# A chain of layers on one core: norms between layers on VectorE alone, their root read from PSUM, and table set-up in smaller steps

## The chip, the core and the metric

The kernel runs on one core of a Trainium2 chip. A core has five engines with instruction queues of their own: PE (TensorE, matrix products), DVE (VectorE) and ACT (ScalarE) for elementwise work, POOL (GpSimd), and SP, which issues DMA transfers. They meet through semaphores. PE writes to PSUM, which DVE and ACT can read and POOL cannot; everything else lies in SBUF. The metric is the time of one execution in microseconds, the median of three runs. PE's clock has two levels, 1.2 and 2.4 GHz; the profile gives the granted clock as a share of full speed.

## The reference

Two blocks of two layers each run one after the other on a sequence of 512 tokens with 1024 channels in float32: a pooling mixer, a gated feed-forward layer with a short convolution (ffn0), windowed attention, a second such feed-forward layer (ffn1), a state-space layer (s5), an MLP (mlp0), a second kind of state-space layer (ssd), an MLP (mlp1) and a last norm. What matters here is what lies between them:

```python
def rms_norm(x, g):
    y = xf * lax.rsqrt(jnp.mean(xf * xf, axis=-1, keepdims=True) + RMS_EPS)
    return y * g
# first block, twice: a norm before, a norm behind
    h = rms_norm(x, mix_pre_g[layer])
    x = x + rms_norm(m, mix_post_g[layer])
    f = conv_glu_ffn(rms_norm(x, ffn_pre_g[layer]), ...)
    x = x + rms_norm(f, ffn_post_g[layer])
# second block, twice: a norm with scale and shift before
    h = _modulate(_rmsnorm(x, norm_mix_g[i]), sh1, sc1)      # h * (1 + scale) + shift
    x = x + g1 * y
    h = _modulate(_rmsnorm(x, norm_mlp_g[i]), sh2, sc2)
    x = x + g2 * _sq_relu_mlp(h, mlp_w1[i], mlp_w2[i])
```

The s5 layer needs tables that depend only on its parameters (powers of complex numbers, phasors, small matrices), and the second block needs modulation vectors (`mod`), products of a condition vector with large matrices.

## The kernel before, in words

The state `xT` is kept transposed: eight tiles of 128 channels x 512 tokens in SBUF. A product with a weight matrix is made of three matmuls (lines 219 to 221): every float32 operand is split into a rounded high part and a low part (ACT writes the high part, DVE the difference), and high x high, high x low and low x high are added up in PSUM. A weight chunk of 128 x 1024 is loaded by SP and split likewise (lines 204 and 205).

**Passages.** `seam` (line 796) joins two layers. For each half of the tokens it issues the last products of the old layer (`tail`), then, with high priority, the chain between them (`chain`, and `run` of the pre-norm), then the first products of the new layer (`head`). There are seven such passages: pool to ffn0, ffn0 to attention, attention to ffn1, ffn1 to s5, s5 to mlp0, mlp0 to ssd and ssd to mlp1.

**Norms.** `Norm.add` (line 283) squares a tile on ACT and adds it to a sum of squares; there are two sums, one added up by DVE and one by POOL, shared out by `engs(k)` (odd tiles to POOL). `Norm.rs` (line 298) takes the sum over channels with matmuls against ones (line 306, both sums accumulated), makes the root on ACT (309) and the reciprocal on DVE (310), spreads it over diagonal matrices (313) and by matmuls over all partitions (319), and copies the result from PSUM to SBUF on ACT (321). The PSUM pool for this, `psn`, has one buffer. `Norm.rs` is called 22 times: eleven norms, two halves.

`post_add` (line 438) is the norm behind a layer of the first block: product with root and gain (lines 449 and 450), addition to `xT` (453), and, where the next layer is of the kind `PreScale`, the split of the result (427, 428), which needs no root since the root is multiplied in after the product. Tiles 2 and 5 are multiplied on POOL (their gain is multiplied in ahead by ACT, line 442), and odd tiles are added on POOL. `PreNorm.run` (line 26) is the norm before a layer of the second block: product with the root (397, alternately on DVE and POOL), scale and shift on DVE (400), rounding on ACT (401), and low part on DVE (402). `staged` issues such steps in a skewed order that `POST_LAGS` and `PRE_LAGS` set.

**Background.** Tables for s5 (`s5_tables`, `s5_powers`, lines 535 to 662), their last part (`s5_toeplitz`) and the modulation (`vecmat`) are generators. `bg[0](n)` takes n steps of each; a step ends at a `yield`. During pool one step is taken behind the first half (line 932). The layer ffn0 takes four steps as its body begins (`bg[0](rate)`, line 998) and four after each pair of column tiles, one after each evacuation of a down projection, and what is left at its end. The layer ffn1 does the same with a rate of three, for the modulation and the last part of the tables.

**Order.** The instructions are written in program order, but a planner that simulates the program sets the order on each engine: by readiness and by priority, which is the place in the program order unless it is raised. Where an engine would be idle in the simulation, it is given later work that is ready. On the chip each engine then runs its queue strictly in that order.

Of the kernel before, what the change touches and what calls it, by code (L numbers as in the profile page):

```python
# [11 lines left out]
F32 = mybir.dt.float32  # L12
# [9 lines left out]
P = 128  # L22
# [9 lines left out]
POST_LAGS = (0, 2, 3, 4)  # L32
PRE_LAGS = (0, 1, 1, 3)
POOL_K = (2, 5)
# [29 lines left out]
def net_kernel(ctx: ExitStack, tc: tile.TileContext, I: dict, out: bass.AP, parts=ALL):  # L64
# [213 lines left out]
    class Norm:  # L278
        def __init__(self):
            self.acc = {}  # L280
            self.seen = set()

        def add(self, tile_, span, eng):
            a, b = span
            if eng not in self.acc:
                self.acc[eng] = tt("acc")
            dst = self.acc[eng][:, a:b]
            if (eng, a) not in self.seen:
                self.seen.add((eng, a))
                if span == FULL:  # L290
                    self.seen.add((eng, HALVES[1][0]))
# [6 lines left out]
        def rs(self, span, eps, out=None):  # L298
# [3 lines left out]
            accs = list(self.acc.values())  # L302
# [11 lines left out]
            if nb == 2:  # L314
                p2 = ps[:, 256:]
            else:
                p2 = psn.tile([P, 512], F32, tag="n", name=nm("pn"))
# [53 lines left out]
    class PreNorm:  # L371
# [15 lines left out]
        def run(self, span):  # L387
# [25 lines left out]
    class PreScale(PreNorm):  # L413
# [21 lines left out]
    def engs(k):  # L435
        return G if k % 2 else V
# [1616 lines left out]
```

## Time and profile before

| | |
|---|---|
| median of three runs | 2519.96 us (2519.84 to 2521.32) |
| profiled execution: its own time | 2522.2 us |
| its span, first to last instruction | 2520.5 us |
| mean granted clock of PE | 0.968 |
| busy: PE, DVE, ACT, POOL | 94%, 68%, 46%, 18% of the span |
| instructions | 33869 |

The busy shares are means over stages with different limits. PE is busy nearly throughout, so what counts is where it stands still or runs at the lower clock, and who is late there. The granted clock falls below 1 in and behind the passages between layers. A row of a timeline gives the start, the time taken by the row's instructions together, the engine, line and operands, and in brackets the idle time of the engine just before, with what ended it. An instruction's duration includes a tail in which the next one can already run, so the distance between two starts is its price where an engine works without a break.

### The profile page before, as it was taken

What the parts mean: (1) busy time and instruction counts of PE and PEld (TensorE: products, weight loads), DVE (VectorE), ACT (ScalarE), POOL (GpSimd) and SP (SyncE); (2) the same over time, 40 slices, a digit from 0 to 9 for tenths busy, and PEclk for the clock granted to TensorE, in tenths of its full rate; (3) what the DMA queues carried; (4) which work ended last, traced back from release to release, by engine and by line L of the source; (5) the groups of instructions that cost most, each with busy time, mean ns of one, the idle gap of its engine ahead of it and who ended that gap; (6) DMA issues with size and microseconds to landing.
All of it is one profiled execution on the core that took longest, in us unless ns stands there. A gap on an engine that the chain in (4) does not pass through costs nothing.

```text
span 2520.5 us, 33869 instructions
## 1 busy us (share of the span) xinstructions
PE 2358.8 (94%) x12485; PEld 1986.4 (79%) x12485; DVE 1717.7 (68%) x2969; ACT 1151.8 (46%) x2070; POOL 454.9 (18%) x489
## 2 busy tenths in 40 slices
PE   6889999988889999996899999999999999999998
PEld 5767777876677888886878887788877888888888
DVE  6895987677858778777654666666778788633333
ACT  6443534467676444354543432333555554422322
POOL 2202131131321000014111210112133432301110
PEclk9989999989999999997999999999999999999999
DMA  4234443312094555551952356543333332233322
GB/s 123 67 100 131 125 138 112 122 43 67 27 231 136 176 175 167 184 176 56 304 158 76 114 167 195 178 149 97 110 101 97 111 103 82 91 100 97 96 88 72
DMA packets 297782, 311.32 MB, mean 124 GB/s; under 512 B 53569, under 2 KB 251025, under 8 KB 296593
## 3 DMA queue, kind: packets, MB, share of 16 engines
q1 hardware_dynamic: 270033, 278.22, 35.5%
q10 hardware_dynamic: 23680, 17.31, 2.3%
q0 software_dynamic: 3904, 13.63, 1.6%
q8 instruction: 98, 1.61, 0.3%
q14 instruction: 67, 0.55, 0.1%
HBM read 284.92 MB, written 24.18 MB: 123 GB/s over the span
## 4 chain that ended last, share of the span: by engine, by line
PE 70%; DVE 12%; DMA 7%; ACT 5%; issue 4%; POOL 1%; SPq 0%; DVEq 0%; ACTq 0%; POOLq 0%
PE mm L220 20%; PE mm L219 20%; PE mm L221 20%; DMA as<-in_ada_w 4%; DVE wl L205 2%; DVE aa L504 1%; DMA tz<-d_k 1%; ACT wh L204 1%; PE pb L1725 1%; PE mm L1655 1%; DVE u L450 1%; PE mm L1656 1%; PE mm L1657 1%; PE pn L306 1%; PE pb L765 1%
## 5 line engine op out<-in xcount | busy, mean ns | idle before, releaser
L219 PE MATMUL mm<-h,wh 128*128 128x512 f32 (+1 forms) x1792 | 665.0, 374 | 40.5 <-DVE u L952 14.2
L220 PE MATMUL mm<-h,wh 128*128 128x512 f32 (+1 forms) x1792 | 668.3, 374 | 24.8 <-DVE h L428 12.6
L221 PE MATMUL mm<-h,wl 128*128 128x512 f32 (+1 forms) x1792 | 665.7, 372 | 1.9 <-DVE wl L205 1.9
L204 ACT ACTIVATE wh<-ws 128x1024 fp32r<-128x1024 f32 (+1 forms) x367 | 387.6, 1059 | 563.7 <-PE mm L220 490.4
L205 DVE TENSOR_TENSOR wl<-ws,wh 128x1024 fp32r<-128x1024 f32 (+1 forms) x367 | 467.2, 1277 | 256.0 <-ACT wh L204 247.6
L219 PEld LDWEIGHTS mm<-h,wh 128*128 128x128 f32 x1792 | 348.0, 195 | 97.6 <-issue 16.9
L220 PEld LDWEIGHTS mm<-h,wh 128*128 128x128 f32 x1792 | 348.3, 195 | 83.6 <-DVE h L428 15.5
L221 PEld LDWEIGHTS mm<-h,wl 128*128 128x128 f32 x1792 | 348.9, 195 | 57.0 <-DVE wl L205 2.5
L219 PE MATMUL mm<-hi,wh 128*128 128x512 f32 (+1 forms) x1056 | 370.9, 356 | 10.1 <-ACT wh L204 9.6
L220 PE MATMUL mm<-lo,wh 128*128 128x512 f32 (+1 forms) x1056 | 371.9, 354 | 1.6 <-DVE lo L328 1.5
L221 PE MATMUL mm<-hi,wl 128*128 128x512 f32 (+1 forms) x1056 | 371.0, 353 | 0.2 <-DVE wl L205 0.2
L219 PEld LDWEIGHTS mm<-hi,wh 128*128 128x128 f32 x1056 | 201.3, 191 | 37.8 <-ACT wh L204 10.9
L220 PEld LDWEIGHTS mm<-lo,wh 128*128 128x128 f32 x1056 | 202.2, 191 | 28.4 <-DVE lo L328 2.6
L221 PEld LDWEIGHTS mm<-hi,wl 128*128 128x128 f32 x1056 | 201.4, 191 | 26.8 <-DVE wl L205 0.7
L504 DVE SCALAR_TENSOR_TENSOR aa<-as,cond,aa 128x512 f32<-128x512 f32 x168 | 130.5, 777 | 113.3 <-DMA as<-in_ada_w 112.1
L1279 POOL TENSOR_TENSOR r<-r 128x512 f32<-128x512 f32 x64 | 85.7, 1343 | 520.1 <-ACT r L1275 445.3
L771 POOL TENSOR_TENSOR dd<-ident,s5dg 16x64 f32<-16x64 f32 x16 | 56.6, 3539 | 327.5 <-DVE kt L773 320.3
L296 POOL TENSOR_TENSOR acc<-acc,sq 128x256 f32<-128x256 f32 (+1 forms) x64 | 58.5, 916 | 302.8 <-ACT sq L295 292.4
L328 DVE TENSOR_TENSOR lo<-r,hi 128x512 fp32r<-128x512 f32 x64 | 47.2, 743 | 76.9 <-ACT hi L326 76.9
L1300 DVE SCALAR_TENSOR_TENSOR x<-mm,mod,x 128x512 f32<-128x512 f32 (+1 forms) x76 | 48.9, 662 | 62.5 <-PE mm L221 62.4
L512 ACT ACTIVATE ab<-aa 128x512 bf16<-128x512 f32 x72 | 45.0, 625 | 89.5 <-DVE aa L504 49.8
L326 ACT ACTIVATE hi<-r 128x512 fp32r<-128x512 f32 x64 | 40.1, 630 | 70.1 <-POOL r L1279 70.1
(491 smaller groups left out, 3822.7 us busy)
## 6 DMA issues: line engine op xcount, KB each, us to landing
ws<-in_mlp_w SPq DMA_DIRECT2D x124, 512.0 KB, 4.0
as<-in_ada_w SPq DMA_DIRECT2D x192, 256.0 KB, 3.1
ws<-in_ffn_w_in SPq DMA_DIRECT2D x88, 512.0 KB, 4.4
ws<-in_m_w_in SPq DMA_DIRECT2D x41, 512.0 KB, 3.7
ws<-in_ffn_w_out SPq DMA_DIRECT2D x40, 512.0 KB, 3.8
ws<-in_w_o SPq DMA_DIRECT2D x16, 512.0 KB, 3.7
ct<-d_tab SPq DMA_DIRECT2D x8, 1024.0 KB, 6.2
ws<-in_s_w_glu SPq DMA_DIRECT2D x16, 512.0 KB, 6.3
```

Source lines behind the costliest of these rows:

```text
L204: A.activation(h_, s_, AF.Copy)
L205: V.tensor_tensor(l_, s_, f(h_), ALU.subtract)
L219: T.matmul(ps, wh, xh, start=first, stop=False)
L220: T.matmul(ps, wh, xl, start=False, stop=False)
L221: return T.matmul(ps, wl, xh, start=False, stop=last).ins
L296: eng.tensor_tensor(dst, dst, sq[:, a:b], ALU.add)
L328: return hi_, V.tensor_tensor(lo[:, ts], src, f(hi[:, ts]), ALU.subtract)
L504: V.scalar_tensor_tensor(acc, st, col(k), acc, ALU.mult, ALU.add)
L512: A.activation(parts[j], acc, AF.Copy)
L771: G.tensor_tensor(dd, ident[:16, :16].unsqueeze(1).broadcast_to([16, 4, 16]), dg[:, g4].unsqueeze(2).broadcast_to([16, 4, 16]), ALU.mult)
L1279: G.tensor_tensor(r, r, r, ALU.mult)
L1300: V.scalar_tensor_tensor(xT[n][:, ts], ps, md(i, 5, n), xT[n][:, ts], ALU.mult, ALU.add)
```

## The change

- **One sum of squares.** `Norm.add` knows no engines any more: all squares are added up by DVE in one sum, and line 306 has half as many matmuls.
- **The root stays in PSUM.** `Norm.rs` returns the spread root in PSUM, in the second half of the tile that holds the sums; the copy on ACT goes. `PreScale.run` still copies it to SBUF, since it is used later. In the other norms the products read it from PSUM, on DVE.
- **Chains on DVE.** POOL takes part in none of these chains. `post_add` loses the gain that ACT multiplied in ahead. In `PreNorm.run` a single instruction multiplies by gain and root, ACT adds the shift and rounds, and one DVE instruction adds the shift and subtracts the rounded part: three steps in place of four.
- **Tables in smaller steps.** `s5_powers` has a `yield` after each exponential, after each wider power, after the repeated squarings and after each doubling of the two phasor tables. The step behind the first half of pool is gone. Bodies of ffn0 and ffn1 begin with two steps (four and three before); ffn0 takes five after each pair (four before).

```diff
-POST_LAGS = (0, 2, 3, 4)
-PRE_LAGS = (0, 1, 1, 3)
-POOL_K = (2, 5)
+POST_LAGS = (0, 1, 2, 3)
+PRE_LAGS = (0, 1, 2)
...
-        def add(self, tile_, span, eng):
+        def add(self, tile_, span):
...
-                eng.tensor_tensor(dst, dst, sq[:, a:b], ALU.add)
+                V.tensor_tensor(dst, dst, sq[:, a:b], ALU.add)
...
-                for i, acc in enumerate(accs):
-                    T.matmul(ps[:, j * P:(j + 1) * P], acc[:, a + j * P:a + (j + 1) * P], ones,
-                             start=i == 0, stop=i == len(accs) - 1)
+                T.matmul(ps[:, j * P:(j + 1) * P], self.acc[:, a + j * P:a + (j + 1) * P], ones, start=True, stop=True)
...
+            out = ps[:, 256:256 + (b - a)]
             for j in range(nb):
-                T.matmul(p2[:, j * P:(j + 1) * P], ones, dg[:, j * P:(j + 1) * P], start=True, stop=True)
-            out = tt("rs") if out is None else out
-            A.activation(out[:, a:b], p2[:, :b - a], AF.Copy)
+                T.matmul(out[:, j * P:(j + 1) * P], ones, dg[:, j * P:(j + 1) * P], start=True, stop=True)
             return out
...
-                return engs(k).tensor_tensor(us[k], xT[k][:, ts], rs[:, ts], ALU.mult)
+                return V.scalar_tensor_tensor(us[k], xT[k][:, ts], self.gs[:, k:k + 1], rs, ALU.mult, ALU.mult)
 
             staged((norm,
-                    lambda k: V.tensor_scalar(us[k], us[k], self.gs[:, k:k + 1], md(i, m, k), ALU.mult, ALU.add),
-                    lambda k: A.activation(self.h[k][0][:, ts], us[k], AF.Copy),
-                    lambda k: V.tensor_tensor(self.h[k][1][:, ts], us[k], f(self.h[k][0][:, ts]), ALU.subtract)),
+                    lambda k: A.activation(self.h[k][0][:, ts], us[k], AF.Identity, bias=md(i, m, k)),
+                    lambda k: V.scalar_tensor_tensor(self.h[k][1][:, ts], us[k], md(i, m, k), f(self.h[k][0][:, ts]),
+                                                     ALU.add, ALU.subtract)),
                    PRE_LAGS)
...
-            self.norm.rs(span, self.eps, out=self.rs)
+            A.activation(self.rs[:, slice(*span)], self.norm.rs(span, self.eps), AF.Copy)
...
-        for k in POOL_K:
-            A.activation(ft[k][:, ts], ft[k][:, ts], AF.Copy, scale=vc(gname, g0 + k))
...
-            if k in POOL_K:
-                return G.tensor_tensor(us[k], ft[k][:, ts], rs[:, ts], ALU.mult)
-            return V.scalar_tensor_tensor(us[k], ft[k][:, ts], vc(gname, g0 + k), rs[:, ts], ALU.mult, ALU.mult)
+            return V.scalar_tensor_tensor(us[k], ft[k][:, ts], vc(gname, g0 + k), rs, ALU.mult, ALU.mult)
...
-        staged((norm, lambda k: engs(k).tensor_tensor(xT[k][:, ts], xT[k][:, ts], us[k], ALU.add)) + parts,
+        staged((norm, lambda k: V.tensor_tensor(xT[k][:, ts], xT[k][:, ts], us[k], ALU.add)) + parts,
...
         exp_exact(dt, scr())
+        yield
...
         exp_exact(er, scr())
+        yield
...
             cmul(pr[:, o], pi[:, o], pr[:, 1:w + 1], pi[:, 1:w + 1], *top, tmp)
+            if w > 1:
+                yield
...
             turn = squared(turn)
+        yield
...
                     turn = squared(turn)
-            yield
+                yield
...
             if hf == 0:
-                with behind(last):
-                    work(1)
                 banded(1)
...
-            bg[0](rate)
+            bg[0](2)
...
-                              lambda: rope_c.update(rope_tables()) if "attn" in names else None, 4)
+                              lambda: rope_c.update(rope_tables()) if "attn" in names else None, 5)
```

## Rows read from the trace of the kernel before

**Rows 1.** The page: busy time by engine (part 1) and the last chain (part 4).

```profile
PE 2358.8 (94%) x12485; PEld 1986.4 (79%) x12485; DVE 1717.7 (68%) x2969; ACT 1151.8 (46%) x2070; POOL 454.9 (18%) x489
...
PE 70%; DVE 12%; DMA 7%; ACT 5%; issue 4%; POOL 1%; SPq 0%; DVEq 0%; ACTq 0%; POOLq 0%
```

**Rows 2.** Who waited for whom, PE: total us, times, longest.

```profile
PE mm L219 <- ACT h L427: 13.7, 5, 4.9
PE pn L306 <- DVE acc L296: 12.9, 5, 5.7
PE mm L220 <- DVE h L428: 12.6, 8, 2.6
PE mm L220 <- DVE h L402: 12.1, 8, 3.1
PE mm L219 <- ACT h L401: 11.4, 5, 2.7
```

**Rows 3.** Timeline of PE, first pairs of ffn0: start, us, instruction, idle before.

```profile
134.97 0.77 PE L219 MATMUL mm<-h,wh 128*128 128x512 f32 x1 [14.16 <-DVE u L952]
135.53 0.63 PE L220 MATMUL mm<-h,wh 128*128 128x512 f32 x1
135.96 0.63 PE L221 MATMUL mm<-h,wl 128*128 128x512 f32 x1
...
143.33 0.39 PE L221 MATMUL mm<-h,wl 128*128 128x512 f32 x1
143.56 0.39 PE L219 MATMUL mm<-h,wh 128*128 128x512 f32 x1
```

**Rows 4.** Busy time of each engine in stretches of ffn0, us (instructions), then PE's clock.

```profile
112.00:145.00 33.00, 18.84 (x71) 15.02 (x70) 32.42 (x113) 7.37 (x10) 0.00 (x0) 0.74 0.21 65
122.85:134.13 11.28, 0.00 (x0) 0.00 (x0) 11.21 (x60) 0.00 (x0) 0.00 (x0) 0.55 0.15 47
260.00:345.00 85.00, 85.00 (x381) 67.14 (x380) 78.33 (x130) 40.15 (x56) 21.80 (x4) 1.00 0.44 134
```

The columns are: stretch and its length, then PE, PEld (weight loads), DVE, ACT, POOL, granted clock, DMA share and GB/s.

**Rows 5.** Timeline of all engines, ffn1 to s5, second half.

```profile
1161.89 1.46 DVE L450 SCALAR_TENSOR_TENSOR u<-f,vec,rs 128x256 f32<-128x256 f32 x2 [3.30 <-ACT rs L321]
...
1165.12 1.77 POOL L453 TENSOR_TENSOR x<-x,u 128x256 f32<-128x256 f32 x2
...
1166.23 0.94 DVE L450 SCALAR_TENSOR_TENSOR u<-f,vec,rs 128x256 f32<-128x256 f32 x1
...
1167.10 0.41 DVE L453 TENSOR_TENSOR x<-x,u 128x256 f32<-128x256 f32 x1
1167.44 0.47 DVE L450 SCALAR_TENSOR_TENSOR u<-f,vec,rs 128x256 f32<-128x256 f32 x1
...
1167.83 0.41 DVE L453 TENSOR_TENSOR x<-x,u 128x256 f32<-128x256 f32 x1
...
1170.89 2.23 PE L306 MATMUL pn<-ones,acc 128*128 128x128 f32 x8 [5.21 <-DVE acc L296]
...
1174.16 1.19 PE L319 MATMUL pn<-dg,ones 128*128 128x128 f32 x4 [1.04 <-DVE dg L313]
...
1175.86 0.42 DVE L397 TENSOR_TENSOR u<-x,rs 128x256 f32<-128x256 f32 x1 [1.65 <-ACT rs L321]
...
1179.74 0.58 PE L220 MATMUL mm<-h,wh 128*128 128x256 f32 x1 [1.42 <-DVE h L402]
```

**Rows 6.** Groups of DVE instructions by shape: count, busy us, mean ns, idle before.

```profile
L1300 DVE SCALAR_TENSOR_TENSOR x<-mm,mod,x 128x256 f32<-128x256 f32 x24 | 10.5, 477 | 27.9 <-PE mm L221 27.9
```

**Rows 7.** Groups of PE instructions by line.

```profile
L306 PE MATMUL pn<-ones,acc 128*128 128x128 f32 x176 | 28.2, 297 | 15.0 <-DVE acc L296 12.9 <-POOL acc L296 1.3 <-ACT rs L321 0.5
```

**Rows 8.** The page, DMA issues (part 6): queue, count, KB each, us to landing.

```profile
as<-in_ada_w SPq DMA_DIRECT2D x192, 256.0 KB, 3.1
```

**Rows 9.** Timeline of all engines, ffn0 to attention, second half.

```profile
531.73 0.26 ACT L309 ACTIVATE sr<-pn,eps 128x2 f32<-128x2 f32 x1 [1.25 <-PE pn L306]
...
537.63 0.47 DVE L450 SCALAR_TENSOR_TENSOR u<-f,vec,rs 128x256 f32<-128x256 f32 x1
```

More of the change, by code (lines that the diff above doesn't have):

```diff
@@ L279, in __init__ @@
         def __init__(self):
-            self.acc = {}
+            self.acc = None
             self.seen = set()
-        def add(self, tile_, span, eng):
+        def add(self, tile_, span):
             a, b = span
[L285 to L289, printed above, removed]
+            if self.acc is None:
+                self.acc = tt("acc")
+            dst = self.acc[:, a:b]
+            if a not in self.seen:
+                self.seen.add(a)
                 if span == FULL:
-                    self.seen.add((eng, HALVES[1][0]))
+                    self.seen.add(HALVES[1][0])
                 A.activation(dst, tile_[:, a:b], AF.Square)
@@ L295, in add, with rs @@
                 A.activation(sq[:, a:b], tile_[:, a:b], AF.Square)
-                eng.tensor_tensor(dst, dst, sq[:, a:b], ALU.add)
-        def rs(self, span, eps, out=None):
+                V.tensor_tensor(dst, dst, sq[:, a:b], ALU.add)
+        def rs(self, span, eps):
             a, b = span
             nb = (b - a) // P
-            accs = list(self.acc.values())
             ps = psn.tile([P, 512], F32, tag="n", name=nm("pn"))
             for j in range(nb):
-                for i, acc in enumerate(accs):
-                    T.matmul(ps[:, j * P:(j + 1) * P], acc[:, a + j * P:a + (j + 1) * P], ones,
-                             start=i == 0, stop=i == len(accs) - 1)
+                T.matmul(ps[:, j * P:(j + 1) * P], self.acc[:, a + j * P:a + (j + 1) * P], ones, start=True, stop=True)
             sr = cst.tile([P, 4], F32, tag="nsr", bufs=2, name=nm("sr"))
@@ L313, in rs @@
                 V.tensor_scalar(dg[:, j * P:(j + 1) * P], ident, sr[:, j:j + 1], None, ALU.mult)
[L314 to L317, printed above, removed]
+            out = ps[:, 256:256 + (b - a)]
             for j in range(nb):
-                T.matmul(p2[:, j * P:(j + 1) * P], ones, dg[:, j * P:(j + 1) * P], start=True, stop=True)
-            out = tt("rs") if out is None else out
-            A.activation(out[:, a:b], p2[:, :b - a], AF.Copy)
+                T.matmul(out[:, j * P:(j + 1) * P], ones, dg[:, j * P:(j + 1) * P], start=True, stop=True)
             return out
@@ L432, in run @@
                 self.rs = xp.tile([P, S], F32, tag="rsx", name=nm("rsx"))
-            self.norm.rs(span, self.eps, out=self.rs)
-    def engs(k):
-        return G if k % 2 else V
+            A.activation(self.rs[:, slice(*span)], self.norm.rs(span, self.eps), AF.Copy)
     def post_add(ft, sq, gname, g0, span, nxt, pre):
         ts = slice(*span)
-        for k in POOL_K:
-            A.activation(ft[k][:, ts], ft[k][:, ts], AF.Copy, scale=vc(gname, g0 + k))
         rs = sq.rs(span, eps1)
@@ L447, in norm @@
             us[k] = tt("u")[:, ts]
-            if k in POOL_K:
-                return G.tensor_tensor(us[k], ft[k][:, ts], rs[:, ts], ALU.mult)
-            return V.scalar_tensor_tensor(us[k], ft[k][:, ts], vc(gname, g0 + k), rs[:, ts], ALU.mult, ALU.mult)
+            return V.scalar_tensor_tensor(us[k], ft[k][:, ts], vc(gname, g0 + k), rs, ALU.mult, ALU.mult)
         parts = pre.parts(span) if pre is not None else ()
-        staged((norm, lambda k: engs(k).tensor_tensor(xT[k][:, ts], xT[k][:, ts], us[k], ALU.add)) + parts,
+        staged((norm, lambda k: V.tensor_tensor(xT[k][:, ts], xT[k][:, ts], us[k], ALU.add)) + parts,
                POST_LAGS[:2 + len(parts)])
         for k in range(KD):
-            nxt.add(xT[k], span, engs(k))
+            nxt.add(xT[k], span)
     def reduce_angle(a, k):
@@ L914, in tail_ @@
             if hf == 0:
-                last = banded(0)
+                banded(0)
             a, b = HALVES[hf]
@@ L928, in tail_ @@
                     A.activation(ft[n + q][:, a:b], o, AF.Copy, scale=vc("pool_scale", n + q))
-                    sq.add(ft[n + q], (a, b), engs(q))
+                    sq.add(ft[n + q], (a, b))
             if hf == 0:
-                with behind(last):
-                    work(1)
                 banded(1)
@@ L993, in down @@
                 if last:
-                    S_["sq"].add(ft[n], span, engs(n))
+                    S_["sq"].add(ft[n], span)
         def body_():
             hh, hl = S_["pre"].hi, S_["pre"].lo
-            bg[0](rate)
+            bg[0](2)
             for ph, (j0, j1) in enumerate(phases):
@@ L1157, in o_proj @@
                     A.activation(ft[n + q][:, slice(*HALVES[th])], o, AF.Copy)
-                    S_["sq"].add(ft[n + q], HALVES[th], engs(q))
+                    S_["sq"].add(ft[n + q], HALVES[th])
         def head(hf, pre):
@@ L1301, in down @@
             if nxt is not None:
-                nxt.add(xT[n], span, engs(n))
+                nxt.add(xT[n], span)
             bg[0](1)
@@ L1441, in glu @@
             if S_["nxt"] is not None:
-                S_["nxt"].add(xT[n], span, engs(n))
+                S_["nxt"].add(xT[n], span)
         def body_():
@@ L1681, in o_evac @@
             if S_["nxt"] is not None:
-                S_["nxt"].add(xT[n], span, engs(n))
+                S_["nxt"].add(xT[n], span)
         def bcast(a, o, d=64):
@@ L1908, in chain @@
             for k in range(KD):
-                nxt.add(xT[k], span, engs(k))
+                nxt.add(xT[k], span)
     work = Background()
```

## The prediction

> **What bounds the kernel now.** The page's first part has TensorE (PE) busy for 94% of the span, and the chain that ended last runs through PE for 70% and VectorE (DVE) for 12% of it [rows 1]. So only what makes PE stand still, or run slowly, can change the time much. The second view is the list of who PE waited for: the five waits that belong to norm chains are 13.7, 12.9, 12.6, 12.1 and 11.4 us, together 62.7 [rows 2]. The third is one large single wait: after the layer between pool and attention (ffn0) has begun, PE stands 14.16 us for line 952, the evacuation of its PSUM tiles [rows 3]. In those 33 us DVE is busy for 32.4, and from 122.85 to 134.13 it runs 60 instructions in 11.2 us, all of the lines 469 to 478, 618 to 623 and 644 to 647, which set up the state-space tables [rows 4]. PE's next matmuls start 0.43 us apart instead of 0.23 [rows 3]: it had been idle and comes back at the lower of its two clocks (1.2 of 2.4 GHz), for 14 matmuls, so 14 x 0.20 = 2.8 us more. That one place costs 17.0 us.
>
> The last view is the timeline of a chain, the second half between ffn1 and s5 [rows 5]. While POOL runs its additions (two in 1.77 us from 1165.12), DVE's line 450 takes 0.94 us. Once it runs alone it takes 0.47, and the next DVE instruction starts 0.39 later (0.34 after a plain addition). So POOL does not give DVE time: what it takes over, it takes from its neighbour.
>
> **The change part by part.** The sum is against the profiled execution, 2522.2 us (span 2520.5 and 1.7 around it); the median of the runs is 2519.96, 2.2 lower, and I take that off at the end. Letters A to G are the seven passages between layers, in order.
>
> (a) Tables in smaller steps. The layer ffn0 began with four steps of tables in one go; now it begins with two small ones, and five follow after each pair of columns. The two are some 42 instructions on 64 columns; the 60 above, many of them wider, are 0.19 us apart in the mean, so at most 8 us, and I take 5.5; before, the block in front of line 952 was at least the 11.2 us above. The next call brings five steps (some 70 instructions, at most 13 us by that spacing, I take 11), the third about 50, 9 us. They stand before later evacuations. A pair of column tiles is 96 matmuls 0.23 us apart, 22 us; in the second phase DVE is busy for 92% of that (78.3 of 85 us [rows 4]), 20 us, with four regular steps in it, each three products on 512 columns, at most 2 x 0.34 each, 2.0 in all. That leaves 12 us for the pair itself: with 11 more it is 23 of 22, with 9 more 21 of 22, and the head's two tiles and the 5.5 us come on top, so I reckon DVE 2 to 5 us late in sum. So of 17.0 us I take -12, the nearer end being the one with little late; the bounds are -17 (all gone) and 0 (the stall moves one pair on).
>
> (b) The first table step leaves the pool stage: two transposes on PE, two Sin activations with a table load on ScalarE (ACT), five loads on SP's queue and the arithmetic on DVE. They pass the second half of pool, passage A and the first weights of ffn0. ACT is busy 7.4 of 33 us where they go [rows 4], which covers them; if the five loads come late, their transposes would hold PE for a load. In the pool stage DVE was the limit, but a planner fills free time with such steps anyway: -3, bounds -6 and +4.
>
> (c) The root read from PSUM, in the pre-norms of D, E (two halves each), F and G (one exposed half each). From the last root matmul (1174.16 + 1.19 = 1175.35) to the matmul that needs the first low part (1179.74) there are 4.39 us [rows 5]: a copy on ACT (the first use starts 0.51 after the matmuls), a product, a second pass, a rounding, a subtraction, all beside POOL. The new order has three products and one subtraction ahead of that matmul, 3 x 0.39 + 0.48 and some 0.15 of signalling, 1.8: 2.6 saved, six times, -15.6. That a DVE instruction reads PSUM costs little: line 1300, the same kind of instruction on 256 columns with PSUM as an input, has a mean of 477 ns [rows 6].
>
> (d) Post-norms, eight halves in A to D. In D the products and sums take from 1161.89 to 1170.89, 9.0 us, then eight matmuls 2.23 [rows 5]. New: 8 x 0.39 + 8 x 0.34 + 7 x 0.34 = 8.2, four matmuls 1.1, and the copy of 0.4 is gone: 2.4 less, twice, -5. In A and B the copy (0.4) and about four instructions a half that are no longer doubled (4 x 0.5) give 2.5, four halves, -10. In C the wait is ACT's, behind transposed tables that wait for DMA: -1. Together -16.
>
> (e) Half of the 176 sum matmuls go. They are busy for 28.2 us in all, 0.16 each [rows 7]; the 72 removed ones that (d) has not counted are worth at most 11.5 us and nothing where PE would wait for the next link anyway. I take -6, the middle.
>
> (f) What DVE gets in exchange. 62 additions move from POOL to DVE; they are 0.34 us each when alone [rows 5], at most 21 us, nearly all beside PE's tail matmuls: +3, bounds 0 and +10. In the second phase of ffn0 DVE is busy 78.3 of 85 us [rows 4] and gets one more table step after each of four pairs, four times 2.0 us: 86.3 of 85, so lateness of +4, bounds 0 and +8. In ffn1 the first call does two steps instead of three, so one more pair of loads for the modulation is left to the end, where each takes 3.1 us to land [rows 8], 6.2 if neither overlaps anything: +2, bounds 0 and +6.
>
> The sum is -12 - 3 - 15.6 - 16 - 6 + 9 = -43.6. The order on every engine comes from a planner that simulates the program, and the 14.16 us above show that its times are not the chip's; chains also share DVE with weight splits. I give back a quarter of (c) and (d), 8 us: -35.6. 2522.2 - 35.6 - 2.2 is 2484.4; I say **2485**.
>
> **The rivals.**
> The PSUM bank is held (0.12). There is one buffer for roots, and it stays occupied until the last of eight products has read it, not until one copy is done. In B the next root's square root already ran at 531.73, while the last product of the current one began at 537.63 [rows 9]; it must now wait some 6 us. The Trainium skill, page PSUM — Partial Sum Buffer, section "PSUM bank collisions raise a hardware error", says that two engines may not touch one bank at the same time, whatever the columns, so that the wait cannot be dodged by using the free half of the tile. By that rule the sum loses what the following root matters; no run here shows a collision. At 6 us for each of the three passages A, B and C, less the 3 or so that DVE needs before it could serve that root, it costs 9 us: 2494.
>
> DVE becomes the bound in ffn0 (0.15). Then the stall comes back in the second or third pair and in the later phases: (a) is nothing and (f) is at its upper bounds, +12 and +15: 2512.
>
> Slower (0.10): DVE instructions stay near 0.9 us although POOL is quiet, because something else (ACT's and PE's reads in the same passages) doubles them. Then POOL's 16 products, 32 additions and 62 sums of squares are an addition to DVE's serial path: (16 + 32) x 0.87 + 62 x 0.34 = 63 us (0.87 is the distance from 1166.23 to 1167.10 [rows 5]); 14 of the 22 half chains are exposed and carry about two thirds, 42, and (c) and (d) shrink to the copies, 14 x 0.4 = 6. 42 - 6 - 12 - 3 - 6 + 9 is +24: 2544. It decides from a mean of about 0.7 us for line 450 and its like upward. Against it: the 0.47 beside an idle POOL [rows 5].
>
> It hardly matters (0.08): the planner puts other ready work into each gap, PE waits for weights instead; within 5 us of 2520.
>
> **How the numbers follow.** 0.55 for the forecast. 0.2%, about what a measurement can tell from no change here, is 5 us. With (a) at -17, (b) at -6, (f) at its lower bounds and nothing given back, the sum is -60.6, so 2460 is the low end; the ffn0 rival at 2512 and part of "hardly matters" set the high end at 2514. Faster than 2515: the forecast, the bank, the ffn0 rival, 0.82, less some for pieces of those that fall short: 0.80. Within 5 us 0.09. Slower 0.11.
>
> **What would show it.** Right: no PE wait over 5 us between 110 and 145; lines 450 and 453 (after: in post_add) at 0.47 and 0.41 in the mean; the root's matmul followed by the first low part within 2 us; norm waits of PE near 30 us instead of 62.7; 88 sum matmuls. Wrong: a new wait for the root's PSUM tile, DVE full and PE waiting in ffn0's second phase, or the mean of the chain's DVE instructions above 0.7 us.

## The result and the profile after

| | before | after |
|---|---|---|
| median of the runs taken side by side (4 each) | 2520.64 us (2519.84 to 2524.68) | 2486.14 us (2484.64 to 2488.75) |
| ratio | | 0.9861, 95% interval 0.9844 to 0.9878 |
| profiled execution, its span | 2520.5 us | 2483.7 us |
| mean granted clock of PE | 0.968 | 0.972 |

The change makes the kernel 34.5 us faster, 1.4%. The forecast was 2485, so the number is right. Whether its reasons are, is another question: the passages did not gain where the prediction put the gain.

The page of the kernel after: busy time by engine (part 1) and the chain that ended last (part 4), as in [rows 1].

```profile
PE 2340.7 (94%) x12397; PEld 1972.1 (79%) x12397; DVE 1713.8 (69%) x3069; ACT 1142.1 (46%) x2038; POOL 337.9 (14%) x345
...
PE 74%; DVE 12%; DMA 6%; ACT 4%; issue 3%; SPq 0%; POOL 0%; DVEq 0%; ACTq 0%; POOLq 0%
```

PE has 88 matmuls fewer, exactly the second sum's. Its busy time fell by 18.1 us and its idle time by 18.7 (161.7 to 143.0). DVE took over POOL's work and is busy no longer than before: its instructions became shorter.

Who waited for whom, PE, in the kernel after: total us, times, longest. These lines answer to [rows 2].

```profile
PE pn L303 <- DVE acc L295: 24.7, 3, 11.9
PE pn L312 <- DVE dg L309: 12.8, 9, 6.1
...
PE mm L218 <- ACT h L418: 7.2, 4, 1.8
PE mm L218 <- ACT h L391: 7.0, 6, 1.5
PE mm L218 <- DVE u L939: 6.1, 1, 6.1
...
PE mm L219 <- DVE h L392: 3.3, 6, 1.2
...
PE mm L219 <- DVE h L419: 2.6, 5, 0.8
```

The waits for a rounded or low part (lines 418, 419, 391, 392) fell from 49.8 to 20.1 us. Against that, the wait for the sum of squares rose from 12.9 to 24.7, and the one for the diagonal (line 309) from 3.3 to 12.8. Two places stand behind these: passage D with 11.9 and 9.4 us (5.7 and 5.2 before), and passage C with 6.1 us, which is new.

How far the kernel after is ahead of the kernel before at the same instruction (its start in either timeline) shows where the time went:

| place | before | after | lead |
|---|---|---|---|
| first product of ffn0 taken out of PSUM (A done) | 95.8 | 84.0 | 11.8 |
| first down projection of ffn0 | 205.0 | 181.4 | 23.6 |
| last activation of ffn0 | 462.1 | 441.6 | 20.5 |
| first output projection of attention | 668.1 | 643.3 | 24.8 |
| last product of the head of ffn1 (C done) | 781.9 | 761.0 | 20.9 |
| last copy of the first down projection, ffn1 | 891.9 | 873.1 | 18.8 |
| first product of s5 (D done) | 1179.7 | 1161.9 | 17.8 |
| last gate of s5 | 1378.0 | 1355.8 | 22.2 |
| first product of mlp0 (E done) | 1392.0 | 1366.7 | 25.3 |
| first product of ssd (F done) | 1762.1 | 1728.8 | 33.3 |
| end | 2520.5 | 2483.7 | 36.8 |

The start of ffn0 brings 12 us, as (a) said. C and D, where (d) and (c) wanted 11 us, bring none: the lead falls from 24.8 to 20.9 over C and from 18.8 to 17.8 over D. From D's end to F's the lead grows by 15.5, twice the 7.8 that (c) put into E and F.

### The profile page after: what moved, and what is told of

It is laid out like the page before. It is cut to its first block, busy times and chain, and to the rows that moved or that the text cites. A ratio compares the mean times of both kernels' runs of the same rounds, so it can differ in the third digit from the quotient of the medians.

```text
span 2483.7 us, 33557 instructions
## 1 busy us (share of the span) xinstructions
PE 2340.7 (94%) x12397; PEld 1972.1 (79%) x12397; DVE 1713.8 (69%) x3069; ACT 1142.1 (46%) x2038; POOL 337.9 (14%) x345
## 4 chain that ended last, share of the span: by engine, by line
PE 74%; DVE 12%; DMA 6%; ACT 4%; issue 3%; SPq 0%; POOL 0%; DVEq 0%; ACTq 0%; POOLq 0%
PE mm L219 22%; PE mm L218 22%; PE mm L220 22%; DMA as<-in_ada_w 3%; DVE wl L204 3%; ACT wh L203 1%; DVE aa L488 1%; PE mm L1642 1%; PE mm L1643 1%; PE mm L1644 1%; PE pb L1712 1%; PE pb L754 1%; DMA tz<-d_k 1%; ACT th L775 1%; DMA d_u<-usc 1%
## 5 line engine op out<-in xcount | busy, mean ns | idle before, releaser
L218 PE MATMUL mm<-h,wh 128*128 128x512 f32 (+1 forms) x1792 | 665.6, 374 | 22.9 <-ACT h L418 7.2
L219 PEld LDWEIGHTS mm<-lo,wh 128*128 128x128 f32 x1056 | 201.4, 191 | 28.5 <-DVE lo L319 2.7
L760 POOL TENSOR_TENSOR dd<-ident,s5dg 16x64 f32<-16x64 f32 x16 | 69.4, 4337 | 343.1 <-DVE kt L762 336.1
L295 DVE TENSOR_TENSOR acc<-acc,sq 128x256 f32<-128x256 f32 (+1 forms) x148 | 62.0, 432 | 16.4 <-ACT sq L294 11.6
```

The lines of the kernel that those rows point to most:

```text
L218: T.matmul(ps, wh, xh, start=first, stop=False)
L219: T.matmul(ps, wh, xl, start=False, stop=False)
L295: V.tensor_tensor(dst, dst, sq[:, a:b], ALU.add)
L760: G.tensor_tensor(dd, ident[:16, :16].unsqueeze(1).broadcast_to([16, 4, 16]), dg[:, g4].unsqueeze(2).broadcast_to([16, 4, 16]), ALU.mult)
```

## The experiments

Every kernel was timed against the kernel before on its own chip, so ratios are what compares across them; on these chips the kernel before took 2526.8 to 2529.6 us, a little more than on the first. One thousandth is 2.5 us. The kernels of one group that say "same chip" can also be compared in us.

### Tables and chains apart

Two kernels split the change: the kernel after with the old table steps, and the kernel before with the new ones.

```diff
# chains alone: the kernel after without the new yields, and
-                banded(0)
+                last = banded(0)
...
+                with behind(last):
+                    work(1)
...
-            bg[0](2)
+            bg[0](rate)
# tables alone: the same lines the other way, in the kernel before
```

Chains alone. 

> The kernel after, with the table steps and their calls as before: only the changes to the norms are left. Prediction's theory (terms add up): it lacks (a) -12, (b) -3 and the table costs of (f), +4 and +2, so it is 9 us above the kernel after, 2495, and the stall at line 939 in front of the first evacuations of ffn0 is back with some 14 us. First rival (tables and chains are worth the same place twice: what the stall gives back, the chains have already): within 3 us of the kernel after, 2486. Second rival (the chains gain little by themselves and the tables are nearly everything): 2510 or more.

Tables alone. 

> The kernel before, with only the smaller table steps, the calls of two and five, and no step in the pool stage. Prediction's theory: -12 - 3 + 4 + 2 = -9 against the kernel before, about 2512, and the wait of PE for line 952 falls from 14.2 us to under 7. First rival (the lead of 11.8 us that the kernel after shows at the start of ffn0 is all of the tables and nothing is given back later): 2505 or less. Second rival (the smaller steps need the chains' relief of DVE, and their work comes late without it): the stall moves to a later pair, 2518 or more.

Measured: chains alone 2499.05 us, ratio 0.9883 (0.9868 to 0.9898); tables alone 2521.43 us, ratio 0.9974 (0.9963 to 0.9984). In us of the kernel before that is -29.5 and -6.6, together -36 against the -35 of the whole: the parts add up, and the chains are four fifths. The prediction had -26.6 and -9. With the chains alone the stall before the first evacuations is there with 13.4 us, with the tables alone the longest wait for that line is 6.3 us. But in the traces the tables alone are 17.0 us ahead at the first down projection and only 3.0 when D is done. Such leads are taken against a trace of the first chip. The kernel after and the two below with other norms ahead of D to G have the same code up to the last copy of ffn1's first down projection, and they lead there by 18.8, 15.2 and 14.7 us; so a lead on another chip is good to some 4 us. Two more runs ask what D takes back.

```diff
-            bg[0](2)
+            bg[0](2 if l == 0 else 3)
```

In the kernel before with the new tables. 

> The kernel before with the smaller table steps in ffn0 and none in the pool stage, but ffn1 begins with three steps as in the kernel before. Theory: what the tables gain up to the first down projection of ffn0 (17.0 us between the two traces) is lost in D because ffn1 began with two steps; with three the wait of PE for the sum in D falls from 11.6 us to about 5.7, and the ratio to the kernel before from 0.9974 to 0.994 or less. Rival: the loss in D has another cause (the order there is laid out anew by any change), and the ratio stays between 0.996 and 0.999 with waits for the sum over 8 us.

In the kernel after. 

> The kernel after, but ffn1 begins with three steps, as before, instead of two. Prediction's theory of (f): one more pair of loads for the modulation is no longer left to the end of ffn1, worth 2 us, 2484, and PE's waits for the sum in passage D (11.9 and 9.4 us in the kernel after, 5.7 and 5.2 before) fall since the drain of the modulation no longer takes DVE and ACT there. Rival: those waits are long because PE has no product left to place there, whatever the modulation does: within 3 us of 2486 and both waits over 8 us.

Measured: with the tables alone the ratio falls to 0.995 (0.9937 to 0.9963), and the longest wait for the sum in D is 5.7 us again instead of 11.6. In the kernel after it is 2492.23 us, 0.9853 (0.9836 to 0.987), not to be told from 0.9861, and PE's two waits for a sum in D are 9.41 and 8.35 us, both over 8 as the rival said. Two steps instead of three at the start of ffn1 cost some 6 us in D with the old chains (0.0024), and little or nothing with the new ones.

### The parts of the chain, each put back alone

The three kernels here ran on the same chip; each is the kernel after with one part as before. The cuts leave out the copies of the root to SBUF (in the first two) and the doubled matmuls of the sums.

```diff
# norm ahead of D to G as before (the lags with it)
-                return V.scalar_tensor_tensor(us[k], xT[k][:, ts], self.gs[:, k:k + 1], rs, ALU.mult, ALU.mult)
+                return (G if k % 2 else V).tensor_tensor(us[k], xT[k][:, ts], rs, ALU.mult)
...
-                    lambda k: A.activation(self.h[k][0][:, ts], us[k], AF.Identity, bias=md(i, m, k)),
+                    lambda k: V.tensor_scalar(us[k], us[k], self.gs[:, k:k + 1], md(i, m, k), ALU.mult, ALU.add),
+                    lambda k: A.activation(self.h[k][0][:, ts], us[k], AF.Copy),
# norm behind A to D as before: POOL_K, the gain on ACT, and
-        staged((norm, lambda k: V.tensor_tensor(xT[k][:, ts], xT[k][:, ts], us[k], ALU.add)) + parts,
+        staged((norm, lambda k: (G if k % 2 else V).tensor_tensor(xT[k][:, ts], xT[k][:, ts], us[k], ALU.add)) + parts,
# two sums of squares as before
-                V.tensor_tensor(dst, dst, sq[:, a:b], ALU.add)
+                (G if e else V).tensor_tensor(dst, dst, sq[:, a:b], ALU.add)
```

The norm ahead. 

> The kernel after with the norm ahead of D, E, F and G as before: root copied to SBUF, product alternately on DVE and POOL, scale and shift on DVE, rounding on ACT, low part on DVE. Prediction's theory (c): 15.6 us, three quarters of it 11.7, are lost again: 2498, ratio 0.991, and the waits of PE for h in these lines grow by that. Rival (PE's products of the first half cover the longer chain, so only the second halves show it): 2490, ratio 0.9875.

The norm behind. 

> The kernel after with the norm behind the layers of A to D as before: root copied to SBUF, tiles 2 and 5 multiplied on POOL with the gain multiplied in ahead on ACT, odd tiles added on POOL. Prediction's theory (d): 16 us, three quarters of it 12, are lost again: 2498, ratio 0.991, and line 434 of the kernel after goes from 472 ns back to about 0.9 us. Rival (what DVE loses in each product beside POOL it gains by the fewer instructions, as D showed in the two traces with 9.0 and 9.2 us for the same stretch): 2489 or less, ratio 0.987 or less.

The sums. 

> The kernel after with two sums of squares again, DVE adding up the even tiles and POOL the odd ones, so 176 matmuls against ones instead of 88. Prediction's theory, (e) -6 and (f) +3 for the additions that moved to DVE: 3 us above the kernel after, 0.1% more of the kernel before than the 0.9861 measured, 0.987. Rival (every matmul left out counts in full, 88 x 0.16 = 14 us, and the additions cost nothing beside PE's work): 2500, ratio 0.992. Second rival (the additions on DVE in a dependent row, 0.53 us apart in the kernel after, hold the chains more than the matmuls did): the same as the kernel after or below it.

Measured: the old norm ahead 2517.65 us, ratio 0.996 (0.9947 to 0.9974); the old norm behind 2494.77 us, 0.9875 (0.9862 to 0.9889); the old sums 2489.14 us, 0.9851 (0.9836 to 0.9865). Against 0.9861 that is 25 us lost, 3.5 us lost (inside the intervals), and nothing lost; on this one chip the first stands 22.9 and 28.5 us above the other two. So nearly all of what the chains gain is in the norm ahead of D to G, and more than the whole of (c); both forecasts for it were too low. The rivals that expected less from (d) and (e) were nearer than the prediction; "every matmul counts in full" was far off.

Why the norm ahead is worth 25 us shows in E. First PE's waits in E's second half, one fence each for the kernel before, the kernel after and the kernel with the old norm ahead.

```profile
1389.77 0.50 PE L219 MATMUL mm<-h,wh 128*128 128x256 f32 x2 [1.82 <-ACT h L401]
1391.99 0.58 PE L220 MATMUL mm<-h,wh 128*128 128x256 f32 x1 [1.72 <-DVE h L402]
```

```profile
1364.48 0.51 PE L218 MATMUL mm<-h,wh 128*128 128x256 f32 x2 [1.12 <-ACT h L391]
```

```profile
1381.35 0.51 PE L218 MATMUL mm<-h,wh 128*128 128x256 f32 x2 [2.17 <-ACT h L394]
1383.56 0.58 PE L219 MATMUL mm<-h,wh 128*128 128x256 f32 x1 [1.71 <-DVE h L395]
```

Then the windows of 10 us around them, in the same order of kernels; the columns are those of [rows 4].

```profile
1380.00:1390.00 10.00, 8.18 (x70) 7.98 (x68) 2.81 (x7) 2.76 (x5) 2.58 (x4) 1.00 0.00 0
1390.00:1400.00 10.00, 8.28 (x50) 8.08 (x50) 6.57 (x18) 3.79 (x11) 1.45 (x2) 0.66 0.01 2
```

```profile
1358.00:1368.00 10.00, 8.75 (x70) 8.29 (x69) 5.53 (x16) 4.93 (x12) 0.00 (x0) 1.00 0.00 0
1368.00:1378.00 10.00, 10.00 (x80) 9.75 (x79) 5.68 (x8) 5.83 (x12) 2.74 (x2) 1.00 0.19 57
```

```profile
1372.00:1382.00 10.00, 7.68 (x63) 7.28 (x61) 3.35 (x8) 2.55 (x5) 2.22 (x3) 0.99 0.01 2
1382.00:1392.00 10.00, 8.44 (x52) 8.45 (x53) 6.14 (x17) 3.79 (x11) 1.02 (x2) 0.67 0.00 0
```

The wait falls from 3.54 to 1.12 us, the 2.4 that (c) reckons with (2.6). But behind the long wait PE runs at its lower clock for a while, and behind the short one at full clock. The second window of the kernels with the long wait still holds a part of that wait (1.7 us in the kernel before), so its 50 matmuls can't be set against the 80 of the other. The stretch just behind the wait shows the price, here in the kernel before:

```profile
1392.00:1397.00 5.00, 5.00 (x23) 5.00 (x24) 4.57 (x14) 3.01 (x10) 0.00 (x0) 0.50 0.02 3
```

PE is busy throughout, at half the clock (0.50 granted), and its 23 matmuls start 0.21 us apart; from 1397 on they start 0.12 apart, and at that rate 23 take 2.8 us. So the lower clock costs some 2.2 us here, nearly as much again as the 2.4 us of waiting. It is alike in the other places. This is the mean granted clock of 10 us from about these waits on, for the first and second half of E, for F and for G: 0.66 in all four with the old norm ahead, and 0.83, 1.00, 0.83 and 0.83 in the kernel after. The length of one wait alone doesn't tell: in F of the kernel after the longest of five small waits is 1.12 us too, and the clock falls there.

Over the whole kernel the old norm ahead costs 17.5 us in waits for its two parts (7.0 + 3.3 in the kernel after, and here):

```profile
PE mm L219 <- DVE h L395: 14.5, 8, 4.1
PE mm L218 <- ACT h L394: 13.3, 6, 2.5
```

PE is busy 2347.5 us in it and 2340.7 in the kernel after, 6.8 us more for the same matmuls. These two traces come from different chips; against the kernel with the old norm behind, on the same chip, the waits differ by 17.8 (10.0 there) and the busy time by 7.1 us (2340.4 there), 24.9 together, where the medians differ by 22.9.

Two more kernels divide this. One keeps four steps, but all arithmetic on DVE and the root in PSUM; the other copies the root to SBUF in every norm.

```diff
# four steps on DVE
-                return V.scalar_tensor_tensor(us[k], xT[k][:, ts], self.gs[:, k:k + 1], rs, ALU.mult, ALU.mult)
+                return V.tensor_tensor(us[k], xT[k][:, ts], rs, ALU.mult)
# root copied
-            return out
+            rs = tt("rs")[:, a:b]
+            A.activation(rs, out, AF.Copy)
+            return rs
```

Four steps. 

> The kernel after with four steps in the norms ahead of D, E, F and G (product with the root; scale and shift; rounding on ACT; low part), but all three arithmetic steps on DVE and the root read from PSUM. The whole of these norms as before gave 0.996 against 0.9861, 25 us. Theory A (POOL's share was the loss: its product takes longer and slows DVE's): most of the 25 us stay gained, ratio 0.987 to 0.989, and the granted clock behind the second half of E stays above 0.8. Theory B (the second pass on DVE and its place in the chain were the loss: one more DVE instruction ahead of each rounding): ratio 0.992 or more, and the clock behind E falls to 0.7 or less, since PE waits some 2 us for line 391 or its like and again for the low part.

Root copied. 

> The kernel after, with the spread root copied from PSUM to SBUF by ACT in every norm, as before; products stay on DVE alone. Prediction's theory: each exposed chain is longer by a copy (0.39 us and about 0.1 of signalling), 14 exposed half chains, 14 x 0.5 = 7 us: 2493. Rival of the held bank: the copy frees the one buffer some 6 us sooner, so what A, B and C lose comes back: 2486 or less, with the waits of PE for the spread of the root (line 312 of the kernel after, 12.8 us) smaller. Third: reading PSUM costs or gives nothing that can be measured, within 3 us.

Measured: four steps 2504.20 us, ratio 0.9909 (0.9893 to 0.9926); root copied 2497.59 us, 0.9879 (0.9863 to 0.9896). Four steps on DVE lose about 12 of the 25 us, so theories A and B share it: about half is the fourth step, half is POOL and the copy. In E its two waits are 1.62 and 0.69 us and the next 10 us have 0.83 granted, between the values of the others. The copy alone costs 4.5 us where 7 were expected, and with the two intervals it may cost nothing. Nothing comes back from the sooner freed PSUM buffer.

### Why C and D do not gain

In D the norm behind ffn1 and the sum for the norm ahead stand on PE's path. The timeline of D's second half in the kernel after answers to [rows 5].

```profile
1145.02 0.60 PE L312 MATMUL pn<-dg,ones 128*128 128x128 f32 x4
1145.66 0.87 DVE L434 SCALAR_TENSOR_TENSOR u<-f,vec,pn 128x256 f32<-128x256 f32 x2 [2.10 <-PE pn L312]
1146.45 0.42 DVE L437 TENSOR_TENSOR x<-x,u 128x256 f32<-128x256 f32 x1
1146.78 0.48 DVE L434 SCALAR_TENSOR_TENSOR u<-f,vec,pn 128x256 f32<-128x256 f32 x1
...
1151.82 3.06 DVE L295 TENSOR_TENSOR acc<-acc,sq 128x256 f32<-128x256 f32 x6
...
1155.03 1.20 PE L303 MATMUL pn<-ones,acc 128*128 128x128 f32 x4 [9.40 <-DVE acc L295]
...
1160.14 0.58 PE L219 MATMUL mm<-h,wh 128*128 128x256 f32 x1
```

And the chain of waits of the same kernel names the sums one by one (start, us, what).

```profile
1152.36 0.42 DVE acc L295
1152.87 0.44 DVE acc L295
1153.40 0.44 DVE acc L295
```

Products and additions go as priced, 0.39 and 0.34 us apart, 16 of them with one sum in 6.2 us. The remaining six sums stand 0.53 us apart, not 0.34: each adds to what the one before has just written, and ACT's squares were ready (its last ends at 1152.35). From the first product to the sum's matmul it is 9.4 us; it was 9.0 with POOL's help. So the copy, the eight matmuls and the norm ahead were saved, and the sum in one row took a part back.

The other part is what PE had to do meanwhile. In the kernel before the sum that roots ffn1's output is made at 1156.45, and products of the first half's head follow it until 1165.68 (the wait of 5.21 us ends at 1170.89).

```profile
1156.45 1.13 PE L306 MATMUL pn<-ones,acc 128*128 128x128 f32 x8 [0.19 <-DVE acc L296]
...
1165.40 0.28 PE L221 MATMUL mm<-h,wl 128*128 128x256 f32 x1
```

In the kernel after that sum is made at 1141.93 and the products end at 1145.18: 2.6 us of products behind the sum instead of 8.1. Of the 9.0 us from the first DVE product to the sum's matmul PE's products covered 3.8 (1161.89 to 1165.68); of the 9.4 us now they cover none, and PE waits 9.40 us where it waited 5.21. A chain that is no shorter has lost its cover; the planner had laid out the order anew.

In C it is ACT. Its timeline in the kernel after, around the root of attention's norm (L305):

```profile
726.03 2.21 ACT L775 ACTIVATE th<-tz 128x1024 f32<-128x1024 f32 x1 [0.83 <-issue]
...
733.74 2.03 ACT L775 ACTIVATE th<-tz 128x1024 f32<-128x1024 f32 x1 [5.50 <-DMA d_tab<-th]
...
736.18 0.26 ACT L305 ACTIVATE sr<-pn,eps 128x2 f32<-128x2 f32 x1 [0.40 <-ACT th L775]
```

A copy of a transposed table has one buffer and waits 5.5 us for the store of the copy before; the root stands behind it in ACT's queue. This kernel moves copy and store to POOL, alone and with two sums:

```diff
-            A.activation(th.rearrange("p g (h t) -> p g t h", h=16), tz.rearrange("p g (t h) -> p g t h", t=8), AF.Copy)
-            nc.scalar.dma_start(dr["tab"][n][:, 3072:], th.rearrange("p g j -> p (g j)"))
+            G.tensor_copy(th.rearrange("p g (h t) -> p g t h", h=16), tz.rearrange("p g (t h) -> p g t h", t=8))
+            nc.gpsimd.dma_start(dr["tab"][n][:, 3072:], th.rearrange("p g j -> p (g j)"))
```

Copies on POOL. 

> The kernel after, but the eight copies of the transposed tables (line 775) are made by POOL, and their stores issued from POOL's queue, so that ACT no longer stands there for the store before (5.5 us idle from 728.2 in the kernel after, while the root of attention's norm, ready to be taken on ACT, waits behind it and PE stands). Theory: passage C of the kernel after loses those 5 to 6 us and the lower clock behind them to ACT's queue, so 2478 to 2480, ratio 0.983, and PE's longest wait for line 309 falls from 6.1 us to about 1. Rival (POOL's copy of 128x1024 beside DVE doubles DVE's instructions in attention and C, as POOL's additions did before): no gain or a loss, ratio 0.986 to 0.989. Second rival (PE then waits in C for the next link, the products and low parts): ratio 0.985 to 0.986.

With two sums. 

> The same with two sums of squares again (DVE and POOL, 176 matmuls against ones). In the kernel with the two sums alone, the root in C stood ahead of the table copy on ACT and no wait of 6 us was there; so the price of the second sum was hidden. Theory: with C equal in both, the second sum costs the 6 us of (e) less 3 of (f), and the ratio is 0.001 to 0.003 above that of the kernel with the copy on POOL and one sum. Rival (the matmuls count in full): 0.005 above. Second rival (the additions on DVE cost as much as the matmuls): equal within 0.001.

Measured, on the same chip: 2484.98 us, ratio 0.9835 (0.9815 to 0.9855), and with two sums 2480.10 us, 0.9813 (0.9794 to 0.9832). In the trace of the first the root runs at 723.04, the longest wait for line 309 is 1.0 us, and C gains: the lead when C is done is 32.1 us where the kernel after had 20.9. The ratio itself can't be told from 0.9861. With two sums it can. Against its twin with one sum it is 4.9 us lower, but the intervals overlap: the second sum's matmuls cost nothing in all that the additions on DVE don't cost too. That is the second run that says so, and in it C has no wait of ACT to hide a price.

That nothing is made of two parts. The traces of these two come from one chip. The kernel with two sums is 1.0 us behind its twin at the last activation of ffn0, 9.2 ahead at the first output projection of attention and 11.9 when D is done, but only 5.2 at the last gate of s5 and 2.8 at the end. The windows from D's end to that gate, first the twin, then the kernel with two sums:

```profile
1160.87:1352.21 191.34, 176.83 (x1098) 158.53 (x1098) 108.95 (x140) 90.91 (x128) 22.51 (x38) 0.98 0.59 185
1148.98:1347.02 198.04, 182.91 (x1107) 164.20 (x1107) 105.74 (x136) 91.20 (x127) 25.81 (x41) 0.95 0.57 178
```

With two sums PE is busy 6.1 us longer there with nine matmuls more, at a lower granted clock. So one sum on DVE costs up to D, and two sums lose after D; why they lose in s5 stays open.

One last kernel combined them, two sums up to D and one from there on:

```diff
+        nxt.two = pre.late
...
-            e = self.n % 2
+            e = self.n % 2 if self.two else 0
```

> The kernel with the table copies on POOL and two sums of squares (0.9813), but only one sum, on DVE, for the norms ahead of D, E, F and G; the norms that belong to A, B and C and the one behind ffn1 keep two. In the traces the kernel with two sums everywhere stood 12 us ahead of the one with one sum when D was done, and the latter took back 9 us of them from D to the end. Theory (in A to C the additions on DVE cost, since DVE is late there for tables and splits; from E on the matmuls cost, since PE has little else to wait for): both advantages add up, 9 us under 2480, about 2471, ratio 0.978. Rival (the two differences are luck of the order in D and cannot be had together): 0.981 to 0.984.

Measured: 2478.08 us, ratio 0.9803 (0.9785 to 0.9822). It lies between the two forecasts, and its interval takes in 0.9813. That the two advantages add up isn't shown. Together these two are the best kernels of the study, some 0.5 to 0.6% below the kernel after.

## Why the prediction was right, step by step

The number is right by luck: (c) brought more than was forecast and (d) and (e) less, by about the same.

**(a), 12 us: right.** The lead grows by 11.8 us at the start of ffn0 (with the tables alone by 10.1, from 6.9 to 17.0). The stall did not go. It moved one pair of columns on (it begins 45.8 us behind A's end, before 25.0) and shrank to about the lateness that the step reckoned with (2 to 5 us), as the kernel after shows on PE, against 14.16 [rows 3]:

```profile
135.87 0.76 PE L218 MATMUL mm<-h,wh 128*128 128x512 f32 x1 [6.06 <-DVE u L939]
```

The sign "no wait over 5 us between 110 and 145" was missed by 1. Of the other signs three came true (DVE's product and addition at 0.47 and 0.42 us, the first low part 1.76 us behind the root's matmul, 88 sum matmuls); "norm waits near 30 us" did not, they are 44.8 (24.7 + 20.1).

**(b), 3 us: too small.** When A is done the tables alone are 6.8 us ahead and the chains alone 1.0. So the step that left the pool stage gives its bound of 6 or a little more, and A's norm behind next to nothing. Both comparisons are across chips, and their sum leaves 4 of the 11.8 us that the kernel after leads by there unexplained.

**(c), 15.6 us, of which 11.7 were kept: the term that was mis-sized; it measures 25.** The chain is as short as forecast: in D's second half from the spread root's matmul (1157.19 + 1.19) to the first low part (1160.14) it takes 1.76 us, forecast 1.8, before 4.39. The waits alone measure 17.5, near the 15.6. What the step left out is the clock, 6.8 us. The prediction priced the lower clock in (a), where PE had stood 14 us, and not here, where two waits of 3.5 us together bring it too. Nothing of (c) had to be given back either.

**(d), 16 us, of which 12 were kept: fell.** Putting it back costs 3.5 us, which can't be told from nothing. In D the sums in one row took 0.53 us and not 0.34 each, and PE's cover went; in C the root stood behind a table copy, where a gain of 1 had been forecast; in A there was nothing to gain. That DVE's product goes back to its own time was right, and clearer than forecast, since no product is slow any more (duration min/median/max in ns, first and last start; the kernel before, then the kernel after):

```profile
L450 DVE SCALAR_TENSOR_TENSOR u<-f,vec,rs x48: 468/926/1065, 55.7 to 1167.4; 128x256 f32<-128x256 f32 x48
L434 DVE SCALAR_TENSOR_TENSOR u<-f,vec,pn x64: 467/472/482, 42.6 to 1150.4; 128x256 f32<-128x256 f32 x64
```

**(e), 6 us, with (f)'s 3 us for the additions: fell.** Twice a kernel with 176 matmuls was no slower than its twin with 88 (0.9851 and 0.9861; 0.9813 and 0.9835). PE's busy time does rise with them, on one chip from 2339.5 to 2350.5 us, but the additions that replace them on DVE cost as much: the two sums gain 11.9 us up to D and lose 9.1 behind it. So the forecast net of 3 us is 0 or less. "Nothing where PE would wait for the next link anyway" was in the step, but no run shows that the matmuls stood in such waits. The step's count is off too: (d) had counted 8 of the 88 matmuls, not 16, so 80 were left and the bound was 12.8, not 11.5.

**(f), ffn0 and ffn1.** ffn0 gives back 3.1 us between its first down projection and its last activation (forecast 4), with DVE busy 78.47 of 85 us from 238 to 323, where [rows 4] have 78.33, so DVE is no bound there. In ffn1 the shorter start costs 6 us, the upper bound, with the old chains, and some 2 us or nothing with the new ones.

So the total came out since (c) brought 13 us more than was kept of it, and (d) and (e) with the additions some 14 less. The sum of the parts put back singly (6.6 + 25 + 3.5 - 2.5) is 32.6 of 35 us.

**The rivals.** The held PSUM bank: freeing it by a copy in every norm did not make the kernel faster, so it cost hardly more than those copies do. The 24.7 us that the sum's matmul waits in the kernel after all end with an addition to the sum, none with a product that reads the root. The bank's own price stays open, and no run shows a collision in one. DVE as the bound in ffn0: its first sign, the stall at a later pair, is there with 6.06 us, but (a) keeps its 12, and PE is busy all of the 85 us from 238 on. DVE instructions near 0.9 us are refuted by the rows above. The planner's unrest, for which 8 us were kept, is real; it lies in C and D and is larger there.

## What to carry to other kernels

A wait on a chain can have two prices, the time that the engine stands and the lower clock behind it; read the second from the granted clock and the spacing of the matmuls in the stretch just behind the wait, without the wait itself, or the wait is counted twice. Before pricing a shorter chain, look at what covered it: a planner that lays out the order anew may take the cover away. Work that is removed from one engine isn't gained if what replaces it on another costs as much. And put parts back one at a time even when the total is right, since errors of opposite sign leave no other trace.

## What the hardware showed that was not expected

**A product that reads the root from PSUM isn't held up by POOL, and an addition with both inputs in SBUF is.** In the kernel after with two sums, POOL adds sums while DVE works on the chain in C (timelines of POOL and of DVE).

```profile
732.95 0.86 POOL L298 TENSOR_TENSOR acc<-acc,sq 128x256 f32<-128x256 f32 x1 [12.18 <-ACT sq L297]
735.08 0.72 POOL L298 TENSOR_TENSOR acc<-acc,sq 128x256 f32<-128x256 f32 x1 [1.27 <-ACT sq L297]
```

```profile
733.12 0.47 DVE L440 SCALAR_TENSOR_TENSOR u<-f,vec,pn 128x256 f32<-128x256 f32 x1
...
735.13 0.95 DVE L443 TENSOR_TENSOR x<-x,u 128x256 f32<-128x256 f32 x1
```

The product lies wholly within POOL's first addition and takes its usual 0.47 us. The addition that begins just after POOL's second has begun takes 0.95 instead of 0.42. In this whole kernel the 64 products of this kind take 0.48 us at most, and the longest of the 64 additions takes 0.97. So the prediction's sentence that POOL's work comes out of DVE's time holds for operands in SBUF, and moving the root to PSUM alone takes the products out of it. In the kernel with the table copies on POOL it is plainer, since POOL's instruction is longer:

```profile
727.89 2.09 POOL L775 COPY th<-tz 128x1024 f32<-128x1024 f32 x1 [6.50 <-DMA tz<-d_k]
```

```profile
728.05 2.04 DVE L437 TENSOR_TENSOR x<-x,u 128x256 f32<-128x256 f32 x1
```

DVE's addition of 0.42 us begins 0.16 behind POOL's copy and ends 0.11 behind it: it was not slowed by a fixed factor, it lasted until POOL was done. The 64 products take 0.49 us at most in this kernel too. The Trainium skill, page SBUF — State Buffer, section "🔬 SBUF: two separate sides", says that the port pair which the two engines share is an exclusive lock for a whole instruction, and that a VectorE operation with two SBUF inputs contends for it with a GpSimd operation that reads SBUF. The rows above agree: the product with one input in SBUF keeps its 0.47 us, and the additions with two last until POOL's instruction is over.

**Additions into one tile in a row cost more than independent instructions of their shape**: in D they start 0.53 us apart against 0.34, at a duration of 0.43 and 0.42. DVE stands idle 0.10 us before each of them, which no duration shows. That it waits for the sum just written is argued from the program; no run tests it alone.
